# Convolution and feed-forward products over all tokens as 2x2 blocks in seven block products, with the combined operands in SBUF slots and DRAM

## Chip, cores and metric

The kernel runs on one core of a Trainium2 chip. The metric is the device time of one execution in microseconds (us); less is better.

## What is computed

Two blocks follow each other on 1024 tokens of 1024 features. `first_block` (two layers, a gated mixing layer and a windowed attention) ends with the normed residual X2. The change concerns `second_block`, which is run with one layer:

```python
def short_conv_mixer(h, w_in, conv_w, w_out, on_grid):
    gate_b, gate_c, hv = jnp.split(h @ w_in, 3, axis=-1)
    u = gate_c * hv
    conv = conv3_grid(u, conv_w) if on_grid else conv3_seq(u, conv_w)
    return (gate_b * conv) @ w_out
...
def swiglu(h, w_in, w_out):
    gate, up = jnp.split(h @ w_in, 2, axis=-1)
    return (jax.nn.silu(gate) * up) @ w_out
...
        hl = modulate(rmsnorm(x, norm1_g[i]), sh1, sc1)
...
        x = x + g1 * yl
        x = x + g2 * swiglu(modulate(rmsnorm(x, norm2_g[i]), sh2, sc2), ffn_w_in[i], ffn_w_out[i])
...
    return rmsnorm(x, final_g)
```

`w_in` of the convolution is 1024x3072 and `w_out` 1024x1024; the feed-forward layer has 2816 hidden features (22 groups of 128), so its `w_in` is 1024x5632 and its `w_out` 2816x1024. `conv3_grid` is a three-tap convolution within rows of 64 tokens.

## The kernel before

Every large product is made in float32r in three matmuls: each operand is split into a high part (ACT casts it, L100) and a remainder (DVE subtracts, L101), and TensorE (PE) adds high by high, high by remainder and remainder by high into one PSUM bank. Weights come page by page: `wpage` loads 512 KB into one of three `raw` buffers (L115, issued by SP), lets POOL multiply it by a gate row where one is given (L117), and splits it into one of four pages `w`. A page is so ready after a load, a cast and a subtraction.

The second block works in two halves of 512 tokens (`tg`), each over

- conv in (L1145 in `by_feature`): 24 groups of 128 features, each 24 matmuls 128x512 over a page; then, on DVE and ACT, the product of the two gates and the convolution (L1171 to L1180);
- conv out (L1196): four pages for each half of the output features, four tiles of 128 tokens; the residual X2 is loaded (L1200), X3 stored, and for the first half of the tokens the normed and transposed input of the feed-forward layer is built (`to_h3`);
- FFN in (L1145 again): 44 groups of features; L1238 to L1240 make the gated product;
- FFN out (L1285): eleven pages for each half of the output features, `end_of` adds the residual and norms.

The operands of the matmuls (features by tokens, both parts) lie in the large tiles H and HB. The input of conv in is built for tiles 0 to 3 within the attention, and for tiles 4 to 7 by `reload_h2`, as steps spread by `mix` over the conv in products of the first half: X2 is loaded back (L1154), normed (L917 to L933), transposed on PE (L136), shifted (L141, L143) and split.

Each engine has one instruction stream in a fixed order, laid out by a scheduler when the kernel is built; SP issues nearly all DMAs, each behind those ahead of it. The attention ends, tile by tile, with the out products (L983), the layer norm (L987 to L1015, on DVE, ACT and POOL) and the store of X2 (L1016).

## Time and profile before

| | |
|---|---|
| time, median of 3 runs | 2709.77 us (2708.3 to 2711.15) |
| profiled execution, span | 2708.1 us, 36954 instructions |
| PE busy (matmuls) | 2665.1 us, 98% |
| DVE busy | 1639.9 us, 61% |
| ACT busy | 1033.3 us, 38% |
| POOL busy | 519.8 us, 19% |
| HBM traffic | 302.82 MB read, 44.89 MB written |

The span runs from the first to the last instruction of the profiled execution; the median of the runs is 1.7 us above it. PE counts as busy from the issue of a matmul to its modelled end, so overlapping matmuls are counted once.

### The profile page before, as it was taken

How to read it: one execution, taken by the hardware profiler on the slowest of the kernel's cores; microseconds unless marked ns; L12 is line 12 of the kernel's file. 1: busy time of each engine (PE TensorE's matmuls, PEld its weight loads, DVE VectorE, ACT ScalarE, POOL GpSimd, SP SyncE). 2: the span in 40 equal slices, each digit the busy share in tenths (PEclk: the TensorE clock that was granted, in tenths of full speed). 3: DMA queues.
4: the chain of work that ended last, by engine and by line, in shares of the span. 5: the costliest groups of instructions: out<-in, count | busy, mean ns of one | idle time of the engine just before them, and what ended most of it. 6: DMA issues, size and time to landing. Idle time of an engine off the chain costs nothing.

```text
span 2708.1 us, 36954 instructions
## 1 busy us (share of the span) xinstructions
PE 2665.1 (98%) x14170; PEld 2294.9 (85%) x14170; DVE 1639.9 (61%) x2751; ACT 1033.3 (38%) x1839; POOL 519.8 (19%) x522
## 2 busy tenths in 40 slices
PE   8999999999999999999999999999999999999998
PEld 5799998879999788888888888888888888888887
DVE  5677775666778765556677876464444355434443
ACT  4323334322223435345556874342232233222222
POOL 2010000010001412213345761000000034100143
PEclk9999999999999999999999999999999999999999
DMA  7454334464444435541374216253453333433322
GB/s 255 140 151 122 99 119 124 123 206 132 134 137 133 146 97 192 176 155 61 89 247 141 82 64 186 87 163 94 132 156 94 101 102 121 152 98 97 94 94 78
DMA packets 348757, 350.11 MB, mean 129 GB/s; under 512 B 13910, under 2 KB 256110, under 8 KB 348066
## 3 DMA queue, kind: packets, MB, share of 16 engines
q1 hardware_dynamic: 340836, 336.74, 40.2%
q10 hardware_dynamic: 7744, 11.01, 1.1%
q8 instruction: 111, 1.82, 0.3%
q14 instruction: 66, 0.54, 0.1%
HBM read 302.82 MB, written 44.89 MB: 128 GB/s over the span
## 4 chain that ended last, share of the span: by engine, by line
PE 85%; DVE 5%; DMA 4%; ACT 2%; issue 2%; POOL 1%; SPq 0%; POOLq 0%; DVEq 0%; ACTq 0%
PE PS L1145 26%; PE PS L510 14%; PE PS L1285 9%; PE PS L597 7%; PE PS L670 5%; PE PS L386 5%; PE PS L1039 3%; PE PS L1196 3%; PE PS L983 2%; PE PS L855 2%; DMA raw<-in_a_w_in 2%; PE PS L889 2%; PE PS L877 2%; PE PS L491 1%; DVE H L101 1%
## 5 line engine op out<-in xcount | busy, mean ns | idle before, releaser
L101 DVE TENSOR_TENSOR w<-raw,w 128x1024 fp32r<-128x1024 f32 x294 | 411.6, 1401 | 414.6 <-ACT w L100 413.9
L100 ACT CAST w<-raw 128x1024 fp32r<-128x1024 f32 x296 | 310.9, 1051 | 806.8 <-issue 305.0
L1145 PE MATMUL PS<-H,w 128*128 128x512 f32 x2688 | 613.1, 389 | 0.7 <-DVE w L101 0.5
L1145 PEld LDWEIGHTS PS<-H,w 128*128 128x128 f32 x2688 | 503.7, 188 | 105.8 <-DVE w L101 1.0
L510 PE MATMUL PS<-H,w 128*128 128x320 f32 x2112 | 320.5, 309 | 0.8 <-DVE TT L519 0.8
L510 PEld LDWEIGHTS PS<-H,w 128*128 128x128 f32 x2112 | 310.8, 188 | 2.9 <-DVE TT L519 1.1
L117 POOL TENSOR_TENSOR raw<-raw,gb 128x1024 f32<-128x1024 f32 x44 | 111.6, 2536 | 520.6 <-DMA raw<-in_ffn_w_out 500.2
L333 POOL TENSOR_TENSOR H<-ACC,H 128x256 fp32r<-128x256 f32 x52 | 51.4, 988 | 609.4 <-ACT H L332 474.3
L314 DVE SCALAR_TENSOR_TENSOR ACC<-raw,CO,ACC 128x512 f32<-128x512 f32 x182 | 134.2, 749 | 21.1 <-DMA raw<-in_ada_w 18.4
L510 PE MATMUL PS<-H 128*128 128x320 f32 x960 | 144.7, 309 | 0.0
L510 PEld LDWEIGHTS PS<-H 128*128 128x128 f32 x960 | 141.1, 188 | 0.5
L597 PE MATMUL PS<-w,H 128*128 128x512 f32 x600 | 141.3, 394 | 0.1
L1145 PE MATMUL PS<-HB,w 128*128 128x512 f32 x576 | 134.8, 396 | 0.0
L1285 PE MATMUL PS<-w,H 128*128 128x512 f32 x576 | 133.4, 390 | 0.0
L597 PEld LDWEIGHTS PS<-w,H 128*128 128x128 f32 x600 | 112.3, 189 | 23.6 <-ACT TT L515 0.2
L1145 PEld LDWEIGHTS PS<-HB,w 128*128 128x128 f32 x576 | 108.1, 188 | 26.1
L101 DVE TENSOR_TENSOR PTR<-PS,PTR 128x512 fp32r<-128x512 f32 x176 | 106.2, 614 | 38.4 <-ACT PTR L100 37.0
L1285 PEld LDWEIGHTS PS<-w,H 128*128 128x128 f32 x576 | 107.9, 188 | 22.5
L386 PE MATMUL PS<-H 128*128 128x512 f32 x510 | 120.9, 391 | 0.0
L864 ACT ACTIVATE s<-s,sm 128x641 f32<-128x641 f32 (+1 forms) x128 | 103.2, 807 | 43.9 <-DVE sm L862 43.3
L100 ACT CAST PTR<-PS 128x512 fp32r<-128x512 f32 x176 | 91.7, 524 | 57.8 <-PE PS L877 53.7
L386 PEld LDWEIGHTS PS<-H 128*128 128x128 f32 x510 | 94.1, 188 | 21.1 <-issue 0.5
(275 smaller groups left out, 4293.4 us busy)
## 6 DMA issues: line engine op xcount, KB each, us to landing
raw<-in_a_w_in SPq DMA_DIRECT2D x96, 512.0 KB
raw<-in_ffn_w_in SPq DMA_DIRECT2D x88, 512.0 KB
raw<-in_ada_w SPq DMA_DIRECT2D x80, 512.0 KB
raw<-in_conv_w_in SPq DMA_DIRECT2D x48, 512.0 KB
raw<-in_ffn_w_out SPq DMA_DIRECT2D x44, 512.0 KB
raw<-in_a_w_out SPq DMA_DIRECT2D x32, 512.0 KB
raw<-in_b_w_in SPq DMA_DIRECT2D x20, 512.0 KB
VY<-in_ada_w SPq DMA_DIRECT2D x16, 512.0 KB
```

Of the source, the lines that this page charges most:

```text
L100: A.copy(hi, src)
L101: turn["split"] = (eng or V).tensor_tensor(lo, src, hif, ALU.subtract)
L117: G.tensor_tensor(rv, rv, scale, ALU.mult)
L314: V.scalar_tensor_tensor(ACC[:, s, :], r[:, j, :], CO[:, c, k:k + 1], ACC[:, s, :], ALU.mult, ALU.add)
L386: T.matmul(ps, HT[0][:, k, ap, t * 128:(t + 1) * 128], w[:, k % 2, :], start=k == 0 and n == 0, stop=k == 7 and n == 2)
L510: T.matmul(pss[h][:, 0:320], w[:, k, :], HT[0][:, k, ap, h * 320:(h + 1) * 320], start=k == 0 and n == 0, stop=k == 7 and n == 2)
L597: turn["mm"] = T.matmul(accs[t], ys[j].r[:, ap * 640 + t * 128:ap * 640 + (t + 1) * 128], wv[:, j, :], start=kp == 0 and j == 0 and n == 0 ...
L670: T.matmul(pss[j], HP[0][:, g + j, k, ap, :], w[:, k % 2, :], start=k == 0 and n == 0, stop=k == 7 and n == 2)
L864: A.activation(out=p[:, :nk + 1], in_=p[:, :nk + 1], func=AF.Exp, scale=-1.0, bias=sm[:, j:j + 1], accum_out=sm[:, 2 + j:3 + j])
L1039: T.matmul(ps, w[:, k, :], HP[0][:, 2 + 4 * tg:6 + 4 * tg, k, ap, :], start=k == 0 and n == 0, stop=k == 7 and n == 2)
L1145: T.matmul(ps, w[:, k, :], act[:, k, ap, :], start=k == 0 and n == 0, stop=k == 7 and n == 2)
L1285: turn["mm"] = T.matmul(accs[t], hr[:, ap, t * 128:(t + 1) * 128], wv[:, j, :], start=kp == 0 and j == 0 and n == 0, stop=kp == NKP - 1 an ...
```

## The change

Conv in, conv out, FFN in and FFN out are no longer made in halves of 512 tokens, but over all 1024 tokens at once, as products of 2x2 blocks: two groups of features (or two halves of the inner dimension) by two halves of the tokens, in seven block products P1 to P7 in place of eight, in Winograd's form of Strassen's scheme.

- *Right operands.* The blocks B11, B21, B12 and the combinations T1 to T4 of the activations (`right_operands`: four subtractions and five remainder parts on DVE for each pair of tiles) lie in seven slots of 4096 words, five in H and two in HB, for the in products. `keep_half` builds and stores (HR2) the conv input of tiles 0 to 6 within the attention; the last tile is built behind it from the stored X2[7].
- *Left operands.* For two groups of weights, `left_operands` loads two pages into a ring of four raw buffers, makes four combinations on DVE, and splits three and a half pages. `ahead` puts P1 and P2 of the first two sets ahead of the rest.
- *Out products.* The activations of the out products are combined by POOL and written to DRAM (`spill`: TC, TF), those of the weights by POOL steps spread over the in products (`sums_steps`: SC, SF). `out_products` reads both back by `wpage`, seven products in the order P1, P6, P2, P7, P5, P4, P3, into pages that are cut out of the slots. In conv out, what P4 and P3 give is finished by `third`: X3 is stored, normed, transposed, and combined into the slots of FFN in.

The matmuls 128x512 of these four products go from 1152 + 384 + 2112 + 1056 = 4704 to 1008 + 336 + 1848 + 924 = 4116.

```diff
--- before.py
+++ after.py
...
+        HR2 = scratch("HR2", 7, [128, D])
+        HR3 = scratch("HR3", 4, [128, D])
+        RIGHTS = ("B11", "B21", "B12", "T1", "T2", "T3", "T4")
+        TC, TF = ({x: dr.tile([n, 128, 512], F32, name=f"{nm}{x}") for x in RIGHTS} for nm, n in (("TC", 4), ("TF", NFF // 2)))
+        SC, SF = ({x: dr.tile([n, 128, 512], F32, name=f"{nm}{x}") for x in ("S1", "S2", "S3", "S4")}
+                  for nm, n in (("SC", 4), ("SF", NFF // 2)))
...
+        def keep_half(xs, half, i):
...
+            if i < 4:
+                split(H2[0][:, half, 0, :, i * 128:(i + 1) * 128], H2[0][:, half, 1, :, i * 128:(i + 1) * 128],
+                      H2[1][:, half, 0, :, i * 128:(i + 1) * 128], h.rearrange("p (k t) -> p k t", k=4))
+            SY.dma_start(HR2[i][:, half * 512:(half + 1) * 512], h)
...
+        ORDER = ("P1", "P6", "P5", "P7", "P2", "P3", "P4")
+        RIGHT = {"P1": "B21", "P2": "B11", "P3": "B12", "P4": "T4", "P5": "T1", "P6": "T2", "P7": "T3"}
...
+        def split_slots(names, where, t, src):
...
+            for s in range(n):
+                A.copy(r[:, s, 0, :, tk], src[:, s * 512:(s + 1) * 512].rearrange("p (k t) -> p k t", k=4))
+            for s in range(n):
+                V.tensor_tensor(r[:, s, 1, :, tk], src[:, s * 512:(s + 1) * 512].rearrange("p (k t) -> p k t", k=4),
+                                f[:, s, 0, :, tk], ALU.subtract)
+        def right_operands(where, t, h1, h2, tmp):
...
+            split_slots(("B12",), where, t, b12)
+            V.tensor_tensor(t1, b22, b21, ALU.subtract)
+            V.tensor_tensor(t2, b12, t1, ALU.subtract)
+            V.tensor_tensor(t3, b12, b22, ALU.subtract)
+            V.tensor_tensor(t4, b11, t2, ALU.subtract)
+            split_slots(("T1", "T2"), where, t, tmp[:, 0:1024])
+            split_slots(("T3", "T4"), where, t, tmp[:, 1024:2048])
...
+        def left_operands(w, c1, c2):
...
+            r1, r2 = next_raw(), next_raw()
+            SY.dma_start(r1.rearrange("p (k n) -> p k n", k=8), rows(w, c1, 128))
+            SY.dma_start(r2.rearrange("p (k n) -> p k n", k=8), rows(w, c2, 128))
...
+            g1, g2, g3 = page(), page(), page()
...
+            def first():
+                split(g1.r[:, 0:1024], g1.r[:, 1024:2048], g1.f[:, 0:1024], r1)
+            def rest():
+                split(pa[:, 0:512], pa[:, 512:1024], paf[:, 0:512], r2[:, 0:512])
+                a11, a12, a21, a22 = r1[:, 0:512], r1[:, 512:1024], r2[:, 0:512], r2[:, 512:1024]
+                V.tensor_tensor(a21, a22, a21, ALU.add)
+                V.tensor_tensor(a22, a12, a22, ALU.subtract)
+                split(g2.r[:, 0:1024], g2.r[:, 1024:2048], g2.f[:, 0:1024], r2)
+                V.tensor_tensor(a12, a21, a12, ALU.subtract)
+                V.tensor_tensor(a11, a11, a12, ALU.subtract)
+                split(g3.r[:, 0:1024], g3.r[:, 1024:2048], g3.f[:, 0:1024], r1)
...
+        def product(st, name, where, start=True):
...
+            for k in range(4):
+                for n, (w, ap) in enumerate(((hi, 0), (hi, 1), (lo, 0))):
+                    turn["mm"] = T.matmul(ps, w[:, k, :], b[:, ap, k, :], start=start and k == 0 and n == 0,
+                                          stop=k == 3 and n == 2, skip_group_check=not start)
...
+        def tail(st, where, c12):
+            st["rest"]()
+            p1, p5 = st["p1"], U(2 + st["i"] % 2)
+            b = product(st, "P6", where)
+            V.tensor_tensor(p1, b, p1, ALU.add)
+            c = product(st, "P5", where)
+            A.copy(p5, c)
+            G.tensor_tensor(p5, p5, p1, ALU.add)
+            d = product(st, "P7", where)
+            V.tensor_tensor(p5, d, p5, ALU.add)
+            if "early" not in st:
+                product(st, "P2", where, False)
+            c = product(st, "P3", where, False)
+            V.tensor_tensor(c12, c, p1, ALU.add)
+            d = product(st, "P4", where, False)
+            V.tensor_tensor(p1, d, p1, ALU.add)
+            return st["c11"], c12, p1, p5
+        def ahead(sets, where):
+            for st in sets:
+                head(st, where)
+            for st in sets:
+                product(st, "P2", where, False)
+                st["early"] = True
...
+        def spill(dst, j, even, odd, tmp):
...
+            for name, x in (("B11", b11), ("B21", b21), ("B12", b12)):
+                SY.dma_start(dst[name][j], x)
+            G.tensor_tensor(t1, b22, b21, ALU.subtract)
+            SY.dma_start(dst["T1"][j], t1)
+            G.tensor_tensor(t2, b12, t1, ALU.subtract)
+            SY.dma_start(dst["T2"][j], t2)
...
+            def s1():
+                SY.dma_start(a, block(2, 2))
+                SY.dma_start(b, block(2, 1))
+                G.tensor_tensor(a, a, b, ALU.add)
+                SY.dma_start(dst["S1"][j], a)
+                SY.dma_start(b, block(1, 2))
...
+            wpages[:] = pages
+            turn["w"] = 0
+            for name in ("P1", "P6", "P2", "P7", "P5", "P4", "P3"):
...
+                def operands(j, n):
+                    x = right[RIGHT[name]][j:j + n].rearrange("j p t -> p j t")
+                    return wpage(x, n, 512), wpage(moving(name, j, n), n, 512)
...
+                for t in range(4):
+                    use(name, t, ps[:, t])
+                mix.tick()
...
-        H2B = [x.rearrange("p (k h t) -> p k h t", k=8, h=2) for x in (HBt.r, HBt.f)]
-        H3 = H2
...
+        c_in, c_out = I["conv_w_in"][0], I["conv_w_out"][0]
+        first = [left_operands(c_in, 1024 + f * 128, 2048 + f * 128) for f in range(2)]
+        ahead(first, N1)
+        xs = U(4, 2)
+        SY.dma_start(xs, X2[7])
...
+        for t in range(4):
+            a, b = pairs_of()
+            SY.dma_start(a, HR2[t])
+            if t < 3:
+                SY.dma_start(b, HR2[4 + t])
+            else:
+                b = U(16, 2)
+            right_operands(N1, t, a, b, U(12, 4))
...
+            spill(TC, j, cvs[0], cvs[1], U(12, 4))
...
+        def third(i, xs, junk):
...
+            rms(RM[:, i:i + 1], MS[:, i, :])
+            xn, hs = next_raw(), next_raw()
+            V.tensor_scalar(xn, xs, RM[:, i:i + 1], None, op0=ALU.mult)
+            for h in range(2):
+                feature_blocks(xn[:, h * 512:(h + 1) * 512], hs[:, h * 512:(h + 1) * 512], h,
+                               lambda k: C2[:, 24 + k:25 + k], lambda k: C2[:, 16 + k:17 + k], PS[:, 4 + t])
+            if i < 4:
+                split_slots(("B11",), N3, t, hs[:, 0:512])
+                split_slots(("B21",), N3, t, hs[:, 512:1024])
+                SY.dma_start(HR3[t], hs)
+            else:
+                h1 = next_raw()
+                SY.dma_start(h1, HR3[t])
+                right_operands(N3, t, h1, hs, U(8, 4))
+        def conv_use(name, t, ps):
...
+            elif name == "P4":
+                xs = xsr()
+                SY.dma_start(xs, X2[t])
+                G.tensor_tensor(xs[:, 0:512], xs[:, 0:512], r, ALU.add)
+                V.tensor_tensor(r, ps, u2, ALU.add)
+                V.tensor_tensor(r, r, gbs[1], ALU.mult)
+                V.tensor_tensor(xs[:, 512:1024], xs[:, 512:1024], r, ALU.add)
+                third(t, xs, r)
...
+        out_products(c_out, 4, TC, SC, slot_pages((2, 4, 3, 5, 1)), conv_use)
...
+        first = [left_operands(f_in, f * 128, (NFF + f) * 128) for f in range(2)]
+        ahead(first, N3)
...
+                spill(TF, f // 2, ys[0], ys[1], U(12, 4))
...
+        FG = RAW.pop()
...
+        out_products(f_out, NFF // 2, TF, SF, slot_pages((0, 4, 3, 1, 6, 5, 2)), ffn_use)
```

Three places of the new order follow. First PE at the end of the attention, before; `L983` are the attention's out products, `L889` its products with the values, `L1145` conv in, and w_144 to w_147 the four weight pages.

```order
L983 MATMUL PS<-w_146,ot_9555 128x512 x6
L889 MATMUL PS<-PTR,H 128x256 x4
L983 MATMUL PS<-w_147,ot_9555 128x512 x6
L1145 MATMUL PS<-H,w_146 128x512 x24
L1145 MATMUL PS<-H,w_147 128x512 x2
L983 MATMUL PS<-KVA,ot_9555 128x512
L983 MATMUL PS<-w_144,ot_9555 128x512
L1145 MATMUL PS<-H,w_147 128x512 x5
L983 MATMUL PS<-KVA,ot_9555 128x512 x5
L983 MATMUL PS<-w_144,ot_9555 128x512 x5
L1145 MATMUL PS<-H,w_147 128x512 x17
```

After, `L998` are the out products, `L941` transposes of `keep_half`, `L1229` the block products, `L1374` the transposes of the last tile, w_177 to w_180 the weight pages, and slots 5 and 6 (T3, T4) lie in HB:

```order
L998 MATMUL PS<-w_179,ot_9588 128x512 x6
L998 MATMUL PS<-KVA,ot_9588 128x512 x6
L998 MATMUL PS<-w_180,ot_9588 128x512 x6
L998 MATMUL PS<-w_177,ot_9588 128x512 x6
L1229 MATMUL PS<-H,w_180 128x512 x12
L1229 MATMUL PS<-H,w_177 128x512 x12
L941 MATMUL PS<-ident,ZX 128x128 x8
L1229 MATMUL PS<-H,w_177 128x512 x12
L1229 MATMUL PS<-H,w_180 128x512 x12
L1374 MATMUL PS<-ident,E 128x128 x8
L1229 MATMUL PS<-HB,w_178 128x512
```

Before, products of conv in stand between those of the attention; now all of them stand behind the last out product, 48 of them ahead of the last tile's transposes, and the next after those reads T3.

Second, SP behind the attention; before, X_126 is the last tile's X2, X_123 to X_125 those of tiles 4 to 6, r_9554 the tile that it is stored from.

```order
L115 DMA raw_150<-in_conv_w_in 128x8x128 x2
L1016 DMA X_126<-r_9554 128x512 x2
L115 DMA raw_148<-in_conv_w_in 128x8x128
L1154 DMA xs_13840<-X_123 128x1024
L1154 DMA xs_13841<-X_124 128x1024
L1185 DMA gb_13855<-GT_138 128x512
L1200 DMA R_13852<-X_119 128x512
```

After, HR_135 to HR_141 are the stored inputs of tiles 0 to 6 and E the working tile:

```order
L1031 DMA X_126<-r_9587 128x512 x2
L952 DMA HR_141<-ZX 128x512
L1193 DMA raw_13955<-in_conv_w_in 128x8x128
L1365 DMA E<-X_126 128x1024
L1391 DMA E<-HR_139 128x1024
L1391 DMA E<-HR_140 128x1024
L1389 DMA E<-HR_136 128x1024
L1193 DMA raw_182<-in_conv_w_in 128x8x128
L1192 DMA raw_181<-in_conv_w_in 128x8x128
L1193 DMA raw_13955<-in_conv_w_in 128x8x128
L1389 DMA E<-HR_135 128x1024
L1391 DMA E<-HR_141 128x1024
```

The last tile's input comes back from X2 (L1365), and all loads of the others (L1389, L1391) stand behind the store of X2[7] (L1031).

Third, DVE from conv out to FFN in; before, the page splits and gated products (L1239) of FFN in follow the last residual at once.

```order
L101 TENSOR_TENSOR w_147<-raw_150,w_147 128x1024
L1203 TENSOR_TENSOR e_13844<-PS,gb_13856 128x512
L101 TENSOR_TENSOR w_144<-raw_148,w_144 128x1024
L1205 TENSOR_TENSOR r_13854<-e_13844,r_13854 128x512
L920 TENSOR_TENSOR RM<-MS 128x1
L921 TENSOR_SCALAR RM<-RM 128x1
L101 TENSOR_TENSOR w_145<-raw_149,w_145 128x1024
L1239 SCALAR_TENSOR_TENSOR e_13844<-e_13844,PS 128x512
L1240 SCALAR_TENSOR_TENSOR e_13846<-e_13844,PS 128x512
L101 TENSOR_TENSOR w_146<-raw_150,w_146 128x1024
```

After, `L1381` is the shift of the transposed input, `L1169` a remainder part of a slot, `L1177` to `L1180` its combinations, `L1212` to `L1216` those of the weights, `L107` a remainder part of the weights, w_177 the page of the first P1:

```order
L1381 TENSOR_SCALAR raw_183<-PS,C_193 128x128
L1169 TENSOR_TENSOR H<-E,H 128x4x128
L107 TENSOR_TENSOR PA<-raw_182,PA 128x512
L1177 TENSOR_TENSOR E<-raw_183,raw_13955 128x512
L1179 TENSOR_TENSOR E<-raw_183 128x512
L1212 TENSOR_TENSOR raw_182<-raw_182 128x512
L1178 TENSOR_TENSOR E<-raw_183,E 128x512
L1169 TENSOR_TENSOR H<-E,H 128x4x128
L1213 TENSOR_TENSOR raw_182<-raw_181,raw_182 128x512
L107 TENSOR_TENSOR w_177<-raw_181,w_177 128x1024
L1180 TENSOR_TENSOR E<-raw_13955,E 128x512
L1169 TENSOR_TENSOR H<-E,H 128x4x128 x2
```

The split of the page that P1 of FFN in reads now stands behind the shifts and nearly all combinations of the last four tiles.

## Rows read from the trace of the kernel before

**Rows 1.** The page's parts 1 and 2: engine shares, and the granted clock.
```profile
PE 2665.1 (98%) x14170; PEld 2294.9 (85%) x14170; DVE 1639.9 (61%) x2751; ACT 1033.3 (38%) x1839; POOL 519.8 (19%) x522
...
PEclk9999999999999999999999999999999999999999
```

**Rows 2.** Windows of the second block: length, busy time by engine, clock, DMA share, GB/s.
```profile
1800.00:2000.00 200.00, 200.00 (x871) 162.66 (x870) 99.22 (x134) 60.71 (x87) 3.20 (x5) 1.00 0.45 134
...
2200.00:2400.00 200.00, 200.00 (x893) 164.54 (x892) 98.44 (x107) 60.22 (x90) 53.24 (x24) 1.00 0.41 127
```

**Rows 3.** Waits of PE from 1640 us to the end: total, times, longest.
```profile
PE PS L136 <- DVE xs L933: 1.8, 1, 1.8
```

**Rows 4.** Timeline of PE around the end of the attention: start, length, line, count.
```profile
1593.55 3.11 PE L1145 MATMUL PS<-H,w 128*128 128x512 f32 x13
...
1624.04 1.33 PE L983 MATMUL PS<-w,ot 128*128 128x512 f32 x5
1625.20 26.94 PE L1145 MATMUL PS<-H,w 128*128 128x512 f32 x118
1653.98 1.09 PE L136 MATMUL PS<-ident,xs 128*128 128x128 f32 x8 [1.84 <-DVE xs L933]
```

**Rows 5.** Line L1145: shortest, median and longest matmul in ns.
```profile
L1145 PE MATMUL PS<-H,w x2688: 387/389/506, 1593.5 to 2579.2; 128*128 128x512 f32 x192
```

**Rows 6.** DVE's groups by shape, 1600 to 2708 us: busy time, mean ns.
```profile
L101 DVE TENSOR_TENSOR w<-raw,w 128x1024 fp32r<-128x1024 f32 x195 | 278.3, 1428 | 330.4 <-ACT w L100 330.0 <-PE PS L1196 0.4
L1240 DVE SCALAR_TENSOR_TENSOR e<-e,PS 128x512 f32<-128x512 f32 x44 | 30.3, 688 | 106.4 <-PE PS L1145 106.3
L101 DVE TENSOR_TENSOR H<-e,H 128x512 fp32r<-128x512 f32 x40 | 27.5, 687 | 8.1 <-ACT H L100 7.9
L143 DVE TENSOR_SCALAR hs<-PS,C 128x128 f32<-128x128 f32 x48 | 18.6, 405 | 15.5 <-PE PS L136 15.0 <-ACT hs L141 0.3
L933 DVE TENSOR_SCALAR xs<-xs,SM 128x1024 f32<-128x1024 f32 x4 | 3.0, 752 | 2.0 <-POOL SM L922 2.0
```

**Rows 7.** POOL's groups by shape, 1600 to 2708 us.
```profile
L1014 POOL TENSOR_TENSOR r<-r,H 128x512 f32<-128x512 f32 x6 | 8.0, 1350 | 6.4 <-ACT r L1013 6.4
```

**Rows 8.** Timeline at the end of the attention: what releases the last tiles.
```profile
1626.31 0.68 DVE L987 CUSTOM_DVE_ANT_0 r<-PS,r 128x512 f32<-128x512 f32 x1
...
1641.22 1.76 SPq L1016 DMA_DIRECT2D X<-r  x2
...
1643.56 1.66 SPq L1154 DMA_DIRECT2D xs<-X  x2
...
1650.35 0.63 ACT L917 ACTIVATE hs<-xs 128x512 f32<-128x512 f32 x1 [8.65 <-DMA xs<-X]
...
1653.18 0.74 DVE L933 TENSOR_SCALAR xs<-xs,SM 128x1024 f32<-128x1024 f32 x1
```

**Rows 9.** Timeline of the first layer's end: a store of 512 KB, and its reader.
```profile
1091.32 0.32 SPq L652 DMA_DIRECT2D X1A<-xs  x1
...
1093.92 0.32 SPq L654 DMA_DIRECT2D xs<-XH  x1
```

**Rows 10.** Timeline of FFN out: a page's load, and POOL beside DVE.
```profile
2236.69 5.08 SPq L115 DMA_DIRECT2D raw<-in_ffn_w_out  x2
...
2239.07 1.05 ACT L100 CAST w<-raw 128x1024 fp32r<-128x1024 f32 x1 [0.21 <-PE PS L1285]
2240.15 1.23 DVE L101 TENSOR_TENSOR w<-raw,w 128x1024 fp32r<-128x1024 f32 x1 [0.48 <-ACT w L100]
2240.49 3.15 POOL L117 TENSOR_TENSOR raw<-raw,gb 128x1024 f32<-128x1024 f32 x1 [4.91 <-DMA raw<-in_ffn_w_out]
...
2245.14 2.42 POOL L117 TENSOR_TENSOR raw<-raw,gb 128x1024 f32<-128x1024 f32 x1 [1.50 <-DMA raw<-in_ffn_w_out]
2245.76 2.87 DVE L101 TENSOR_TENSOR w<-raw,w 128x1024 fp32r<-128x1024 f32 x1 [4.38 <-ACT w L100]
```

**Rows 11.** Timeline of PE, first layer: a wait and the products behind it.
```profile
54.13 2.50 PE L386 MATMUL PS<-w,H 128*128 128x512 f32 x5 [3.66 <-DVE H L101]
```

**Rows 12.** Windows around that wait (columns as in rows 2).
```profile
54.00:56.00 2.00, 1.86 (x4) 1.50 (x5) 2.00 (x5) 1.80 (x6) 0.00 (x0) 0.50 0.62 156
...
58.00:60.00 2.00, 2.00 (x13) 1.28 (x12) 0.18 (x1) 0.44 (x3) 0.00 (x0) 0.65 0.65 239
60.00:62.00 2.00, 2.00 (x19) 1.37 (x17) 1.69 (x3) 2.00 (x3) 0.00 (x0) 1.00 0.02 8
```

**Rows 13.** Timeline of the tail: the last products, and the last store's issue.
```profile
2699.45 1.56 PE L1285 MATMUL PS<-w,HX 128*128 128x512 f32 x6
```

More of the change, by code (lines that the diff above doesn't have):

```diff
@@ L922, in rms @@
             G.tensor_tensor(dst, dst, mhalf[:, 0:1], ALU.pow)
-        def into(h, t):
-            return lambda k0, n: tuple(x[:, k0:k0 + n, j, t * 128:(t + 1) * 128]
-                                    for x, j in ((h[0], 0), (h[0], 1), (h[1], 0)))
         def normed_h2(i, xs, dst, hsr):
@@ new lines, in head @@
+        def head(st, where):
+            st["first"]()
+            st["p1"] = U(st["i"] % 2)
+            ps = product(st, "P1", where)
+            A.copy(st["p1"], ps)
+            st["c11"] = ps
+        def tail(st, where, c12):
[15 more added lines that the diff above has]
+            return st["c11"], c12, p1, p5
@@ new lines, in program @@
+        cvr = ring([U(4 + 2 * i, 2) for i in range(3)])
+        steps = [x for j in range(4) for x in sums_steps(c_out, j, SC, U(16), U(17))]
+        mix.begin(steps, 11)
+        for j in range(4):
+            cvs = []
+            for f in (2 * j, 2 * j + 1):
+                if f < 2:
+                    st = first[f]
+                else:
+                    st = left_operands(c_in, 1024 + f * 128, 2048 + f * 128)
+                    head(st, N1)
+                u, cv = U(10, 2), cvr()
+                c11, c12, c21, c22 = tail(st, N1, u[:, 512:1024])
+                V.tensor_tensor(u[:, 0:512], c11, c21, ALU.mult)
+                V.tensor_tensor(u[:, 512:1024], c12, c22, ALU.mult)
+                V.tensor_scalar(cv, u, cw[:, 8 + f:9 + f], None, op0=ALU.mult)
@@ new lines, in program, with fourth @@
+        mix.end()
+        FG = RAW.pop()
+        turn["raw"] = 0
+        SY.dma_start(FG, I["final_g"].partition_broadcast(128))
+        for m in range(2):
+            SY.dma_start(gbs[m], GT[4][m, :].partition_broadcast(128))
+        xsr = ring([U(12, 2), U(14, 2)])
+        late = [U(12, 2), U(14, 2), U(8, 2), U(10, 2)]
+        def fourth(i, xs):
+            rms(RX[:, i:i + 1], MS[:, i, :])
+            for h in range(2):
+                c = slice(h * 512, (h + 1) * 512)
+                V.scalar_tensor_tensor(xs[:, c], xs[:, c], RX[:, i:i + 1], FG[:, c], ALU.mult, ALU.mult)
+                SQ("l").dma_start(out[0, i * 128:(i + 1) * 128, c], xs[:, c])
```

395 lines of the change are left out of this document (227 added, 168 removed).

## Prediction

> **What bounds the kernel now.** I read the page's shares first: PE is busy for 98% of the span, DVE for 61, and the granted clock stands at the upper of its two levels, 2.4 GHz, in all forty slices [rows 1]. An average over stages does not tell what the second block alone is bound by, so the windows come next: from 1800 to 2400 us PE is busy without a gap, while DVE has half its time free, POOL a quarter at most in use, and the DMAs move 127 to 134 GB/s [rows 2]. The waits of PE from 1640 us to the end agree: the longest is 1.8 us [rows 3]. The second block is bound by the count of its matmuls, and whatever else it does is hidden.
>
> What a matmul is worth must be read with care. Its own record says 389 ns [rows 5], but matmuls overlap: 118 of them take 26.94 us [rows 4], that is 0.2283 each; I use 0.2285. The second block's 4704 matmuls are then 1075 us.
>
> The end of the attention is the place at which other work is covered. 55 conv in matmuls stand there between the attention's own from 1593.55 us on (13 in the first of six such rows), and the last out product ends at T0 = 1625.2 [rows 4]. Behind T0 the span is accounted for: 4649 matmuls (1062.3), twelve groups of eight transposes like the one at 1653.98 (1.03 each, 12.4), and 8.2 of waits and tail. The tail is 7.1 of these, from the end of the last products (2701.0) to 2708.1 [rows 13].
>
> **Removed.** 588 matmuls, 134.4 us. This is the whole gain. By the record's 389 ns it would be 229, which the row of 118 excludes. From T0 on 4116 are left instead of 4649: -121.8. T0 itself: the 55 matmuls (12.6) can no longer stand ahead of it, since P1's pages are the last two that the out products use; three more groups of transposes for tiles 4 to 6 enter (+3.3), and I give 2.3 for the attention's own short waits that the 55 filled: T0 moves by -7 (bounds -12.6 and 0). The 12.4 of transposes behind T0 now fall into the waits below, and the old 8.2 goes out, to be put in anew.
>
> **Added: three places where PE waits for DVE.** Before, all that feeds the next products was spread under products of the other half of the tokens. With all tokens in one product that cover is gone: nothing of conv in beyond P1 and P2 of two sets can run before the last tile is there, and so at each turn. The prices are those of DVE's steps: 0.687 for a 128x512 subtraction, 0.405 for a shift, 0.75 for a scaling of 128x1024 [rows 6], and 1.23 for a page's remainder when POOL is idle [rows 10].
>
> *Attention to conv in.* The 48 matmuls ahead take 11 us, so PE runs dry at about T0 + 13. The last tile's chain of before: its sums start 1.1 us behind T0, its store is issued at 1641.22, T0 + 16; the load behind it is issued at 1643.56 and lands at 1650.35, 6.8 us later, and the tile is scaled by 1653.9 [rows 8]. A store is followed by its reader after 2.6 us [rows 9]. After, with no page splits of conv in between, I put the store at T0 + 14, the load at +16.6, its landing at +23.4, the scaled tile at +27, and the shifted features at +31 (transposes 1.1, four shifts on DVE for each pair of halves, ACT beside it). `right_operands` is nine DVE steps for each of four pairs, 36; by the order six stand ahead of that point and 30 behind: 20.6 us, to +51.6. The stored tiles' loads stand behind the last store on SP and go into two working pairs, so that the second use of a pair waits for the first: one load of 6.8, nearly all of it, shows: +6, to +57.6. The matmuls that come next read T3 of all tiles, so PE starts there: a wait of 45 us (bounds 36, without the loads and with the store at +12, and 55, with two loads).
>
> *P4 to P3 in conv out.* `third` of tiles 0 to 3 stands ahead of P3 on PE by its 32 transposes, and it borrows the raw buffers that P3's pages need. For each tile DVE makes three steps on the product (2.07), the scaling (0.75), four shifts (1.62), two remainders (1.37) and two small ones (0.3): 6.1, with four tiles and P3's four pages 29.4 us. P3 has only 11 us of matmuls, and ends 43.5 behind P4's end T4 instead of 11: 33 us (bounds 25, if POOL's and ACT's links and the loads into the raws are all covered, and 40).
>
> *Conv out to FFN in.* `third` of tiles 4 to 7 is 4.7 + 6.2 (`right_operands`) = 10.9 us of DVE each, 43.7 in all; with two sets of left operands 56.7 stand in the order from P3's results to the last split that the first sets need. The split that P1 waits for (w_177) comes after 44.2 of them. Some 8 us run before P3 ends, and ACT, POOL and the loads of HR3 add 2: P1 starts at 38 if DVE is undisturbed. It is not: POOL has about 13 steps here, six or seven of which I let DVE wait for.
>
> How much that costs, the trace shows: a remainder of a page takes 1.23 us when POOL starts behind it, and 2.87 when it runs beside POOL's product of 2.42 [rows 10]; the mean over all is 1.43 [rows 6]. POOL's 128x512 step takes 1.35 [rows 7]. DVE reads PSUM in the gated product and stays at 0.688 [rows 6]. I take 8 us, so a wait of 46 (bounds 38 and 56: no collision, or all 13 in full). The Trainium skill, "SBUF — State Buffer", section "Who interferes with whom", says that a DVE step with two SBUF inputs and a GpSimd step that reads SBUF exclude each other for a whole instruction; the 2.87 agrees. By that rule all 13 could count, 56, against the 46 that I take from the mean of the rows.
>
> **Added: smaller terms.** The clock: after a wait of 3.66 us five matmuls take 2.50 us [rows 11], and the windows show 0.50 of full speed, 1.2 GHz, from 54 us, 0.65 until 60, then full speed [rows 12]; some 2.6 us are lost at each restart, three times 8 (bounds 0 and 16). Behind the first and third wait DVE still has left operands to make, 7.1 us a set (3 x 1.23 and 5 x 0.687); I let PE wait 4 of it twice, 8 (bounds 0 and 14). FFN out begins with pages whose load (2236.69 to 2240.49, 3.8), cast (1.05) and remainder (1.23) [rows 10] sum to 6.1; half of it shows, 3. The tail has two scalings in a row on DVE and two more steps in place of one: 8.5. Conv in to conv out has its first pages ready: nothing, covered by 11 us of matmuls for each P.
>
> The in products themselves: a set is 84 matmuls, 19.2 us of PE. DVE has 14.6 us in a gate set of the convolution and 12.6 in one of FFN in (three page remainders and thirteen steps of 0.687), so PE stays the bound if POOL's four to five steps a set cost DVE no more than 4.6 to 6.6 us. They come to 5 to 6.7 when each is waited for in full; with the rows' mean they cost half. I allow 4 us in all.
>
> **The sum** against the profiled span: 2708.1 - 7 - 121.8 - 12.4 - 8.2 = 2558.7; with 45 + 33 + 46 it is 2682.7; with 8 + 8 + 3 + 8.5 + 4 it is 2714.2. The median lies 1.7 above the span, so 2716. The change gives back in three waits what the seventh product saves.
>
> **Rivals.**
> *DVE is undisturbed and early (faster).* The links beside DVE's own counted work (loads of the stored tiles in the first wait, raws in the second, POOL in the third) are all covered, since loads can be issued early and POOL's steps can fall into DVE's waits for ACT. For it speaks that of 195 page remainders the mean is only 0.2 above the free 1.23. Price: 45 becomes 42.5, 33 becomes 25, 46 becomes 38: 2716 - 18.5 = 2697. It decides from where the three waits sum to less than 112 us, 12 below my 124.
> *POOL makes DVE the bound in the in products.* If each POOL step costs DVE its 1.35 and one cast of 1.05 shows in each set, a set of FFN in is 12.6 + 6.75 + 1.05 = 20.4, 1.2 above PE's, 26 over 22 sets; the eight gate sets, 14.6 + 5 + 1.05, add 11: 2716 - 4 + 37 = 2749. For it speaks the 2.87; against it, that PSUM readers, half of DVE's steps, stay at their price.
> *FFN out is paced by the loads.* It has 84 pages, twelve for each P, at twice the pace of before, on three buffers. A buffer goes round in 3.8 + 1.05 + 1.23 and some 0.3, 6.3 us, so twelve pages of a P take 25 us against PE's 30.2. With loads of 6.8, as at the end of the attention [rows 8], it is 9.4 and 38: 8 for each of seven P, less what the first pages bring, +53: 2769. Against it: at 127 GB/s the load took 3.8, and FFN out needs some 190.
> *The waits are hidden after all* and the plain saving stays: 2575. The order speaks against it: PE has no products to put there.
>
> **How the numbers follow.** The forecast 2716 (its own range 2704 to 2732) has 0.38, DVE early 0.32, POOL as the bound 0.17, loads 0.10, the plain saving 0.03. No change means within 0.2%, 2704.4 to 2715.2, about what a measurement of this kernel can tell. Of the forecast 0.13 falls within it and 0.25 above; of DVE early 0.28 below and 0.04 within; with the others: faster 0.31, same 0.17, slower 0.52. The range: all three waits at their lower bounds (99) and no clock or slip term give 2716 - 25 - 16 = 2675, the loads as pace 2769; I take 2672 to 2771, which leaves out the plain saving and the far ends of the waits.
>
> **What the profile after would show.** PE with three gaps of some 45, 33 and 46 us, each ended by a DVE remainder part (a slot's in the first, a page's in the others), the granted clock low behind each; 0.2285 us a matmul between them; PE's share down to about 94%; POOL busier by some 100 us. Wrong would be: gaps of less than 30 (the order does not bind where I think), a string of short waits for DVE in FFN in (POOL as the bound), waits for loads in FFN out, or a clock that stays low for longer than the few microseconds behind a gap.

## The result, and the profile after

The changed kernel takes 2787.54 us (median of four runs, 2781.8 to 2789.81) against 2709.07 before: a ratio of 1.0284, with an interval of 1.0269 to 1.0298. The forecast was 2716, with a range of 2672 to 2771. The profiled execution is the fastest of the four, 2781.8 us with a span of 2780.0.

From the page of the changed kernel, the busy times of the engines and the granted clock in forty slices; for the kernel before these are [rows 1]:

```profile
PE 2575.1 (93%) x13582; PEld 2206.0 (79%) x13582; DVE 1881.4 (68%) x3075; ACT 1080.5 (39%) x1911; POOL 675.0 (24%) x660
...
PEclk9999999999999999999999979999769999999997
```

PE has lost 90 us of busy time and five points of its share, POOL has gained 155 us, and the granted clock now dips. Where PE waits from 1600 us on (total, times, longest):

```profile
PE PS L1229 <- DVE E L1251: 35.1, 11, 7.8
PE PS L1374 <- DVE raw L1445: 20.3, 7, 9.0
PE PS L1374 <- ACT raw L1379: 17.1, 7, 7.2
PE PS L1229 <- ACT HB L1167: 15.6, 1, 15.6
PE PS L1229 <- ACT w L106: 14.2, 2, 12.1
PE PS L1335 <- ACT H L106: 13.9, 2, 11.8
...
PE PS L998 <- ACT ZX L946: 3.7, 3, 1.9
PE PS L941 <- DVE ZX L934: 2.6, 1, 2.6
```

Before, the longest of these waits was 1.8 us [rows 3], and the next was

```profile
PE PS L1196 <- ACT hs L141: 1.4, 1, 1.4
```

The largest sum now, 35.1 us behind DVE's L1251, is none of the three waits of the forecast: 24.7 of it stand in FFN in and 10.4 in conv in. PE's timeline shows where each stands (idle time and what ended it in brackets; rows chosen from 1620 us on):

```profile
1621.55 3.27 PE L998 MATMUL PS<-w,ot 128*128 128x512 f32 x12
...
1639.20 7.35 PE L1229 MATMUL PS<-H,w 128*128 128x512 f32 x24 [7.44 <-ACT E L1238]
...
1655.17 1.97 PE L1374 MATMUL PS<-ident,E 128*128 128x128 f32 x8 [8.63 <-DVE E L1370]
1672.70 1.22 PE L1229 MATMUL PS<-HB,w 128*128 128x512 f32 x2 [15.56 <-ACT HB L1167]
...
1771.50 5.01 PE L1229 MATMUL PS<-HB,PA 128*128 128x512 f32 x12 [7.85 <-DVE E L1251]
...
1963.12 16.51 PE L1335 MATMUL PS<-H 128*128 128x512 f32 x72
...
2013.42 3.33 PE L1335 MATMUL PS<-H 128*128 128x512 f32 x6 [11.79 <-ACT H L106]
...
2025.83 1.54 PE L1335 MATMUL PS<-HB 128*128 128x512 f32 x6
...
2070.78 1.22 PE L1229 MATMUL PS<-H,w 128*128 128x512 f32 x2 [12.10 <-ACT w L106]
...
2134.54 4.45 PE L1229 MATMUL PS<-H,PA 128*128 128x512 f32 x12 [2.85 <-DVE E L1251]
...
2204.10 5.42 PE L1229 MATMUL PS<-H,PA 128*128 128x512 f32 x12 [4.50 <-DVE E L1251]
...
2361.70 2.96 PE L1229 MATMUL PS<-H,PA 128*128 128x512 f32 x12
...
2380.98 2.96 PE L1229 MATMUL PS<-H,PA 128*128 128x512 f32 x12
```

The last two rows are the same product of two successive sets of FFN in, behind all waits: a set then takes 19.28 us. Cut at the places where one group of products ends and the next begins, the span compares with the forecast as follows. The forecast's column is its own sum, stretch by stretch, with 2.6 us for the clock put beside each of the three waits; the last column is an experiment that is told below.

| stretch | matmuls x 0.2285 | forecast | measured | all mends |
|---|---|---|---|---|
| to the last out product of the attention | | 1618.2 | 1624.7 | 1628.3 |
| conv in, with the wait ahead of it | 230.3 | 281.9 | 286.4 | 275.5 |
| conv out, with the wait ahead of P3 | 76.8 | 112.4 | 116.3 | 118.1 |
| wait for P1 of FFN in | | 48.6 | 43.4 | 37.3 |
| FFN in | 422.3 | 430.3 | 467.5 | 430.0 |
| FFN out | 211.1 | 214.1 | 209.9 | 208.9 |
| tail, from the last product | | 8.5 | 31.9 | 18.2 |

The stretches with the three waits came within 5 us of the forecast, though the first of them by two errors that cancel (see below). Two stretches did not: FFN in (37 us more; some 35 if the clock's 2.6 behind the third wait are counted here, where they fell) and the tail (23). They are what the experiments are about.

### The profile page after: what moved, and what is told of

It is laid out like the page before. It is cut to its first block, busy times and chain, and to the rows that moved or that the text cites. A ratio compares the mean times of both kernels' runs of the same rounds, so it can differ in the third digit from the quotient of the medians.

```text
span 2780.0 us, 36848 instructions
## 1 busy us (share of the span) xinstructions
PE 2575.1 (93%) x13582; PEld 2206.0 (79%) x13582; DVE 1881.4 (68%) x3075; ACT 1080.5 (39%) x1911; POOL 675.0 (24%) x660
## 4 chain that ended last, share of the span: by engine, by line
PE 63%; DMA 16%; DVE 8%; POOL 5%; ACT 4%; issue 3%; SPq 1%; POOLq 0%; DVEq 0%; ACTq 0%
PE PS L516 15%; PE PS L1229 13%; PE PS L603 7%; PE PS L392 6%; PE PS L676 5%; DMA E<-in_ffn_w_out 4%; PE PS L1053 3%; PE PS L998 3%; PE PS L861 2%; PE PS L1335 2%; PE PS L895 2%; PE PS L883 2%; DMA raw<-SFS 2%; DVE H L107 2%; DMA E<-in_conv_w_out 2%
## 5 line engine op out<-in xcount | busy, mean ns | idle before, releaser
L1229 PE MATMUL PS<-H,w 128*128 128x512 f32 x1776 | 418.1, 393 | 22.4 <-ACT w L106 14.2
L1229 PEld LDWEIGHTS PS<-H,w 128*128 128x128 f32 x1776 | 336.7, 190 | 96.1 <-ACT w L106 15.4
L106 ACT CAST w<-raw 128x1024 fp32r<-128x1024 f32 x202 | 211.5, 1050 | 396.7 <-PE PS L1229 140.9
L107 DVE TENSOR_TENSOR w<-raw,w 128x1024 fp32r<-128x1024 f32 x200 | 266.7, 1338 | 117.2 <-ACT w L106 115.8
L516 PEld LDWEIGHTS PS<-H,w 128*128 128x128 f32 x2112 | 310.8, 188 | 3.0 <-DVE TT L525 1.2
L107 DVE TENSOR_TENSOR H<-raw,H 128x1024 fp32r<-128x1024 f32 (+1 forms) x133 | 166.4, 1262 | 123.0 <-ACT H L106 121.1
L1335 PE MATMUL PS<-H 128*128 128x512 f32 x924 | 216.0, 392 | 14.0 <-ACT H L106 13.9
L106 ACT CAST H<-raw 128x1024 fp32r<-128x1024 f32 (+1 forms) x133 | 134.1, 1018 | 233.0 <-DMA raw<-in_a_w_in 68.8
L1335 PEld LDWEIGHTS PS<-H 128*128 128x128 f32 x924 | 173.8, 189 | 52.7 <-ACT H L106 14.7
L1229 PE MATMUL PS<-HB,w 128*128 128x512 f32 x672 | 166.7, 401 | 16.7 <-ACT HB L1167 15.6
L1229 PEld LDWEIGHTS PS<-HB,w 128*128 128x128 f32 x672 | 128.0, 191 | 48.3 <-ACT HB L1167 16.0
L320 DVE SCALAR_TENSOR_TENSOR ACC<-raw,CO,ACC 128x512 f32<-128x512 f32 x182 | 133.8, 747 | 20.5 <-DMA raw<-in_ada_w 17.8
L516 PEld LDWEIGHTS PS<-H 128*128 128x128 f32 x960 | 141.1, 188 | 0.5
L603 PE MATMUL PS<-w,H 128*128 128x512 f32 x600 | 140.0, 391 | 0.1
L1251 DVE TENSOR_TENSOR E<-PS,E 128x512 f32<-128x512 f32 x34 | 23.5, 691 | 162.9 <-POOL E L1249 121.9
L107 DVE TENSOR_TENSOR PTR<-PS,PTR 128x512 fp32r<-128x512 f32 x176 | 106.2, 613 | 36.5 <-ACT PTR L106 35.0
L603 PEld LDWEIGHTS PS<-w,H 128*128 128x128 f32 x600 | 111.5, 188 | 23.4 <-ACT TT L521 0.2
L392 PE MATMUL PS<-H 128*128 128x512 f32 x510 | 120.9, 391 | 0.0
```

The lines of the kernel that those rows point to most:

```text
L106: A.copy(hi, src)
L107: turn["split"] = (eng or V).tensor_tensor(lo, src, hif, ALU.subtract)
L320: V.scalar_tensor_tensor(ACC[:, s, :], r[:, j, :], CO[:, c, k:k + 1], ACC[:, s, :], ALU.mult, ALU.add)
L392: T.matmul(ps, HT[0][:, k, ap, t * 128:(t + 1) * 128], w[:, k % 2, :], start=k == 0 and n == 0, stop=k == 7 and n == 2)
L516: T.matmul(pss[h][:, 0:320], w[:, k, :], HT[0][:, k, ap, h * 320:(h + 1) * 320], start=k == 0 and n == 0, stop=k == 7 and n == 2)
L603: turn["mm"] = T.matmul(accs[t], ys[j].r[:, ap * 640 + t * 128:ap * 640 + (t + 1) * 128], wv[:, j, :], start=kp == 0 and j == 0 and n == 0 ...
```

## Experiments

A kernel was run once in most of them, on chips on which the kernel before took 2708 to 2715 us; so the stretches are compared rather than the totals. In the runs that leave a stretch as it was it still varies: FFN in from 467.4 to 471.4 us, the tail from 31.4 to 34.5.

### FFN in: three theories of one wait

The windows of the changed kernel show that the loss is in the part of FFN in in which the weight sums are made (columns as in [rows 2]):

```profile
2120.00:2340.00 220.00, 195.35 (x797) 156.90 (x796) 121.91 (x156) 56.13 (x75) 85.53 (x61) 0.94 0.57 184
2340.00:2500.00 160.00, 160.00 (x699) 130.80 (x698) 117.02 (x134) 51.17 (x69) 36.66 (x24) 1.00 0.32 106
```

Until 2340 us PE is idle for 25 us; behind that, when the last sums are stored, it is busy throughout. What stands ahead of the wait at 2204.10, from the timeline of all engines:

```profile
2196.07 1.29 POOL L1291 TENSOR_TENSOR E<-E 128x512 f32<-128x512 f32 x1 [5.61 <-DMA E<-in_ffn_w_out]
...
2200.84 1.26 POOL L1296 TENSOR_TENSOR E<-E 128x512 f32<-128x512 f32 x1 [3.48 <-DMA E<-in_ffn_w_out]
2202.06 1.26 POOL L1249 TENSOR_TENSOR E<-E 128x512 f32<-128x512 f32 x1
...
2203.36 0.69 DVE L1251 TENSOR_TENSOR E<-PS,E 128x512 f32<-128x512 f32 x1 [10.30 <-POOL E L1249]
```

L1249 adds P5 and P6 of the set in hand. It stands on POOL behind two steps of the weight sums (L1291, L1296) that each wait for a load; DVE's L1251 waits 10.30 us for it, holds up all that is behind it on DVE, and PE waits for the bank that L1251 reads. The theories: A, this order on POOL's queue; B, the port that DVE and POOL share; C, SP's queue, on which weight pages stand behind stores that wait for POOL.

**P5's sum on DVE.**

```diff
-            G.tensor_tensor(p5, p5, p1, ALU.add)
+            V.tensor_tensor(p5, p5, p1, ALU.add)
```

> Only the sum of the fifth product and the sixth (one 128x512 addition for each set of the in products, L1249) goes from POOL to DVE. Theory A (POOL's queue): that sum stands on POOL behind steps of the weight sums that wait for their loads, so DVE's addition behind it, and PE's next product in that bank, wait for a load that has nothing to do with them; the waits of PE for DVE's L1251 (35 us in the profile after) vanish, with what the clock loses behind them: about 40 us less, a span of 2736 to 2745. Theory B (shared port): DVE loses its time to POOL's steps, which all remain, and DVE gets 34 more steps of 0.69: no gain, 2778 to 2790. Theory C (SP's queue: the weight pages come late behind stores that wait): no gain either.

The span is 2755.2 us. FFN in takes 449.9 instead of 467.5, conv in 279.9 instead of 286.4; PE's waits behind L1251 fall to

```profile
PE PS L1229 <- DVE E L1251: 15.0, 5, 4.2
```

The gain of 25 us in all lies between what A expected (40) and what B and C did (none). A holds for 17.6 us of FFN in, but not for all: 26 us above 22 sets of 19.28 stay.

**Weight sums without POOL's additions.**

```diff
-                G.tensor_tensor(a, a, b, ALU.add)
+                if add:
+                    G.tensor_tensor(a, a, b, ALU.add)
```

(the same for the three subtractions; `add` is false in the feed-forward layer.)

> In the feed-forward layer the sums of the weights are not added on POOL: the loads and stores remain in their order, the 44 additions are left out (the output is then of other weights). Theory A (POOL's queue behind loads): nothing on POOL waits for those loads any more, so FFN in runs at PE's 19.3 us a set: about 32 us less, 2745 to 2752. Theory B (shared port): the same 44 steps are gone, 44 x 1.3 us of DVE's waits at most: 20 to 35 less. Theory C (SP's queue): the stores still wait on SP for their loads, ahead of the weight pages: less than 10 us gained. This run tells C from the others, the run with the sum on DVE tells A from B.

The span is 2755.3 us, above A's 2745 to 2752, as conv out took 6 us longer in this run; FFN in takes 434.5, 33 less. A and B both allow that. What C expected did not come, but without additions a store on SP no longer waits for POOL either, so the run is no clear test of C.

**The weight sums' DMAs on POOL's queue, besides P5's sum on DVE.**

```diff
-                SY.dma_start(dst["S1"][j], a)
-                SY.dma_start(b, block(1, 2))
+                G.dma_start(dst["S1"][j], a)
+                G.dma_start(b, block(1, 2))
...
```

> As the run with the sum of P5 on DVE, and the loads and stores of the weight sums are issued by POOL in place of SP. With the sum on DVE FFN in still took 449.9 us from its first to its last product, against 424 for 22 sets at 19.28. Theory C (SP's queue: the weight pages wait behind the sums' stores, which wait for POOL): FFN in takes 424 to 432, and conv in loses a few us too. Theory B (shared port): no change against 450, since all steps of POOL remain.

The span is 2754.0 us. Conv in gains 7 more (273.1), FFN in nothing (454.7), which looked like B. The wait for P1 of FFN in fell as well, to 37.2 us; no run here tells why. But the waits of SP, ACT and PE in FFN in speak against B:

```profile
SPq L1279 <- POOL E L1278: 134.1, 6, 27.9
...
ACT w L106 <- DMA raw<-in_ffn_w_in: 67.2, 6, 16.1
...
PE PS L1229 <- ACT E L1238: 12.7, 4, 3.9
```

SP now stands up to 27.9 us before the stores of `spill`, whose combinations (L1278) are behind the sums on POOL, and ACT waits up to 16.1 us for weight pages that SP has not yet asked for. Behind these casts on ACT stands its copy of P1 (L1238), and PE waits for the bank that this copy reads.

**The stores of `spill` on POOL's queue too.** This was run on the kernel with the feed-forward part alone (below), whose FFN in is the same, and in the kernel with all mends.

```diff
-                SY.dma_start(dst[name][j], x)
+                G.dma_start(dst[name][j], x)
...
-            SY.dma_start(dst["T1"][j], t1)
+            G.dma_start(dst["T1"][j], t1)
```

> The mended feed-forward kernel, and the stores of the combined activations (spill) are issued by POOL too, so that nothing but weight pages stands on SP in FFN in. There FFN in still took 453 us for 22 sets of 19.28 (424), and SP waited 115 us for the first of POOL's combinations. Theory C (SP's queue): 424 to 435. Theory B (shared port, or DVE's and ACT's own work): 445 or more.

FFN in falls from 453.4 us (457.4 in another run of the same FFN in, on the chip of this run) to 431.1. ACT's waits for weight pages of FFN in, ahead of this step (the largest row) and behind it (the only one left):

```profile
ACT w L104 <- DMA raw<-in_ffn_w_in: 65.4, 6, 16.6
```

```profile
ACT PA L104 <- DMA raw<-in_ffn_w_in: 1.9, 1, 1.9
```

C is shown for this part, and B is not the bound: POOL's steps all remain. Each of these gains is that of a step in this order; the stores of `spill` were not moved alone.

### The tail

**The late residuals into the raw buffers.**

```diff
-        late = [U(12, 2), U(14, 2), U(8, 2), U(10, 2)]
+        late = [None, None, None, U(8, 2)]
...
+                if t == 0:
+                    for q in range(4):
+                        if q < 3:
+                            late[q] = next_raw()
```

> In FFN out the residual tiles of the last four tiles of tokens are loaded into the three raw buffers, free once P3's last pages are split, and one working tile, instead of tiles that P4's last results hold until they are stored. Theory D (buffers): the 31.9 us from the last product to the end are a chain of loads that wait for buffers (the last three loads are issued 5 to 11 us behind the last product): 10 to 18 us less, 2762 to 2770. Theory E (work): DVE's and POOL's steps of the last eight tiles alone fill the tail: less than 5 us gained, 2775 to 2781.

The tail is 26.9 us, 5 less, between D and E (the span, 2785.5, has other differences of several us ahead of it and lies above both). The loads that now came late were those of P4's third and fourth tile.

**Four residual tiles for P4 as well.**

```diff
-        xsr = ring([U(12, 2), U(14, 2)])
+        xsr = ring([U(12, 2), U(14, 2)] + XT)
...
```

(XT are two tiles in the space of PA; the late residuals are in the raw buffers, as above.)

> As the run with the residuals in raw buffers (late tiles in the raw buffers), and PA's 2048 words, idle in FFN out, become two more residual tiles, so that P4's four tiles no longer share two. That run left a tail of 26.9 us, in which the loads of P4's third and fourth tile were issued only behind the stores of the first two. Theory D' (P4's ring of two sets the tail): from the last product to the end 10 to 16 us, against 31.9 in the changed kernel. Theory E (work of DVE and POOL): 22 or more.

The tail is 25.0 us, against an expectation of 10 to 16 by theory D': the buffers were not the main part. DVE's timeline shows where else to look:

```profile
2739.45 1.29 DVE L107 TENSOR_TENSOR H<-raw,H 128x512 fp32r<-128x512 f32 x2
...
2740.65 1.28 DVE L1559 TENSOR_TENSOR E<-PS,E 128x512 f32<-128x512 f32 x2
```

DVE comes to the first of P4's results (L1559) only when the last page of P3 is split (L107), 17 us before the last product, and has eight tiles to finish from there.

**P3's last pages behind P4's steps.**

```diff
-                got = [(j, n, *operands(j, n)) for j, n in last]
+                with tc.issue_after(turn["p4"].ins) if last and "p4" in turn else nullcontext():
+                    got = [(j, n, *operands(j, n)) for j, n in last]
```

> The mended feed-forward kernel, and in FFN out the remainder parts of P3's last pages are queued on DVE behind the three steps of each of P4's tiles, which stood behind all of P3's pages: there DVE came to P4's results some 8 us before PE was done though they had been ready for 20, and worked on eight tiles until the end. Theory H (the order of DVE's queue makes the tail): the tail falls from 24.1 us to 10 to 16. Theory E (DVE's work on the last four tiles fills it in any order): 20 or more. If P3's last pages come late instead, FFN out grows beyond 209 by what the tail loses.

The tail is 20.5 instead of 24.1 us, at the end that theory E gave; FFN out stays at 208.9. DVE came to P4's results 28 us ahead of the last product instead of 22 (not 8, as the expectation had it). With `spill` on POOL's queue the same edit takes the tail from 23.4 to 17.0. So the buffers are worth 7 to 10 us (31.9 to 25.0 here, 34.5 to 24.1 in the feed-forward kernels below) and the order 4 to 6. The rest is argued, not tested: in the tail of 17.0 us DVE works on the last tiles for 11.8 us, nearly without a wait, and the last stores land behind that. In the kernel with both parts and all mends the tail is 18.2 us; it was never brought to the 8.5 of the forecast.

### What sets the third wait

**Without the remainder parts of the last four tiles.**

```diff
-            for s in range(n):
+            for s in range(n if lo else 0):
                 V.tensor_tensor(r[:, s, 1, :, tk], src[:, s * 512:(s + 1) * 512].rearrange("p (k t) -> p k t", k=4),
```

> Between conv out and FFN in, the 20 remainder parts (five for each of the last four tiles, 0.687 us each, 13.7 us of DVE) of the combined right operands are left out; those parts of the slots keep old values. Theory F (DVE's counted work sets this wait, as predicted): the stretch from P3's last product to P1 of FFN in shrinks from 43.6 us by 11 to 14. Theory G (the chain of loads, transposes and ACT steps sets it, and DVE's steps lie beside): it shrinks by less than 5.

The wait for P1 falls from 43.4 to 34.8 us: 8.6 for 13.7 us of DVE's work left out, between the two theories.

```profile
2028.56 1.54 PE L1335 MATMUL PS<-HB 128*128 128x512 f32 x6
...
2064.91 1.22 PE L1229 MATMUL PS<-H,w 128*128 128x512 f32 x2 [10.69 <-ACT w L106]
```

DVE's steps are part of this chain, but not all of it; ACT's shifts end some of PE's waits between conv out's P4 and FFN in (17.1 us in the list above). What sets the first two waits was not tested by a run.

### One part alone, and all mends

**The feed-forward part alone.** Conv in and conv out are those of before, in halves of tokens; the input of FFN in is put into the slots tile by tile behind each product of conv out (the edit is shown against the kernel before).

```diff
...
+        N3 = {"B21": 0, "B11": 1, "B12": 2, "T1": 5, "T2": 6, "T3": 3, "T4": 4}
...
         for tg in range(2):
             for fc in range(8):
                 gb_, gc_, hv_ = [by_feature(rows(c_in, base + fc * 128, 128), (H2B if tg else H2)[0]) for base in (0, 1024, 2048)]
...
+                        to_h3(xs, t, tg)
...
```

> One part alone: conv in and conv out as before the change, in halves of 512 tokens; FFN in and FFN out by seven block products. 396 of the 588 matmuls are saved. By the ledger of the changed kernel: 2708 - 90.5 (396 x 0.2285), + 46 for the wait between conv out and FFN in and its clock, + 44 for FFN in behind the weight sums, + 24 for the tail: 2731 (2715 to 2745). Rival (the wait is as dear as all three together, since conv out's last half now carries the work): 2760 or more.

The time is 2719.27 us (the kernel before on that chip 2713.06), within the range expected. FFN in (474.6) and the tail (34.5) lose as in the changed kernel, but the wait ahead of P1 is only 16.8 us, not 46: the next tile's 24 matmuls run while DVE combines the last one.

**The same with the first mends** (P5's sum on DVE, the sums' DMAs on POOL's queue, the residual tiles).

> The feed-forward part alone by block products, with three mends: the sum of P5 on DVE, the weight sums' DMAs on POOL's queue, four residual tiles and the late ones in raw buffers in FFN out. If the causes named so far are the whole loss: 2708 - 90.5 + 46 + 5 + 6 = 2675 (2665 to 2690), 20 to 40 us faster than the kernel before. If the losses only move elsewhere: 2700 or more.

The time is 2687.08 us, near the upper end of what was expected; FFN in was still 453.4, which led to the run with the stores of `spill`.

**Both parts, all mends.**

> The changed kernel with all mends: P5's sum on DVE, all DMAs of the weight sums and of the combined activations on POOL's queue, four residual tiles and late ones in the raw buffers, and P3's last pages behind P4's steps. If its excess over the forecast lay in these queues: 2780 less 13 in conv in, 6 at the third wait, 15 to 35 in FFN in, 8 to 18 in the tail, that is 2708 to 2738, no faster than the kernel before, since three waits remain. Rival (the waits, too, came from the queues): below 2700.

The span is 2716.3 us and the time 2718.12, 0.3% above the kernel before (2710.32 on that chip); its stretches are the last column of the table. In FFN in PE is now idle nowhere between 2120 and 2340 us, with POOL and DVE busier than in the changed kernel:

```profile
2120.00:2340.00 220.00, 220.00 (x959) 179.89 (x958) 186.46 (x197) 67.75 (x91) 128.41 (x153) 1.00 0.57 179
```

**The feed-forward part alone, all mends.**

> Feed-forward part alone with all mends: 2687 less what the two runs beside it gain (8 to 14 in the tail, 0 to 25 in FFN in): 2650 to 2680, 1.2 to 2.4 per cent faster than the kernel before.

The time is 2658.93 us (median of four runs, 2657.71 to 2662.0) against 2710.32: a ratio of 0.9813, interval 0.9796 to 0.9829. It is the fastest version here, 1.9% faster than the kernel before. From its page, the busy times of the engines, and its one long wait:

```profile
PE 2582.1 (97%) x13774; PEld 2221.8 (84%) x13774; DVE 1844.1 (69%) x3001; ACT 1067.2 (40%) x1891; POOL 664.2 (25%) x769
```

```profile
1997.54 5.06 PE L1220 MATMUL PS<-H,w 128*128 128x512 f32 x11 [16.83 <-ACT E L1354]
```

## Why the prediction was wrong

**The step that failed** is "I allow 4 us in all" for the in products. It asked only whether DVE and POOL have enough time in a set, and they have. It did not ask what stands behind what on the queues. The trace before had no step on POOL that waits for a load while PE waits for POOL's next step: in FFN out a multiplied page is a page that PE needs anyway. The change put both on one queue, and its stores ahead of the weight pages on SP. FFN in took 37 us more than forecast: six waits of PE for L1251, 24.0 us, and some 12 for the clock behind them. P5's sum on DVE gave back 17.6, the stores of `spill` off SP's queue 22 to 26, and with both, and the sums' DMAs on POOL's queue, PE had no wait left and FFN in took 430.0. That this is the forecast's 430.3 to a us is luck: the forecast had allowed 8 us for DVE, and what stands there is mostly the clock behind the third wait.

The prediction's own sign of this, "a string of short waits for DVE in FFN in", did appear, but not for the reason of the rival that it stood for. That rival priced POOL's steps (26 us for FFN in); in the kernel with all mends the same steps run and PE does not wait.

**The second** is the tail of 8.5 us, worked out from one tile's chain of before. In the changed kernel P4 and P3 leave eight tiles to the end, since each holds four banks until its last page. 31.9 were measured; buffers and the order of DVE's queue explain a part, and the work of these tiles probably the rest.

**T0 was moved by 0.5 us and not by 7.** From 1200 us to T0 the waits of PE sum to 17.7 us against 10.4 before, 7.3 more, where I had set 2.3; 6.3 stand at the added transposes (the last two rows of the list of waits). That leaves 1.5 of the 6.5 us open, less than the 4 us by which T0 varies between the runs with this attention (1624.7 to 1628.5). No run tests it.

**The first wait was smaller, and conv in came out right by luck.** PE waited 32.8 us in four pieces in place of the one of 45, below its lower bound of 36, and the first product with T3 started 48 us behind T0 instead of 58. But 10.4 us behind L1251 in conv in, and more restarts of the clock than one, made up for it: 286.4 against 281.9. With these waits mended conv in took 275.5. The 48 matmuls ahead did not run in one go, as the forecast had them: behind the first 24 PE waited 7.44 us for ACT's copy of P1 (L1238), which itself waited for the store of X2[7]:

```profile
1638.56 1.07 ACT L1238 COPY E<-PS 128x512 f32<-128x512 f32 x2 [1.19 <-DMA X<-r]
```

**What held.** The other two waits: from P4's end to P3's 48.1 us against 43.5 (of which the counted steps and P3's own matmuls give only 40; the prediction shows no row for the rest), and 43.4 and 2.1 us for FFN in against 46. Their last and longest pieces, 11.79 and 12.10 us, were ended by ACT's casts (L106), not by a DVE remainder part as forecast; in the third, DVE's remainder parts were worth 8.6 us of their 13.7. The price of a matmul: FFN out's 924 took 209.9 us. That FFN out is not paced by loads: PE does not wait there.

The shared port as the bound did not come true: with POOL busy for 128 of 220 us and DVE for 186, PE had no wait. The port does cost DVE time. From 2080 to 2500 us of the changed kernel the 14 steps of L1213 that no step of POOL overlapped took 0.69 us, the six beside one 1.66 to 1.67, and L1255, which reads PSUM, took 0.68 beside POOL too. That PSUM readers keep their price the prediction had taken from a stretch in which POOL hardly worked. One such pair:

```profile
2188.70 1.76 POOL L1307 TENSOR_TENSOR E<-E 128x512 f32<-128x512 f32 x1 [6.40 <-DMA E<-in_ffn_w_out]
...
2189.35 1.66 DVE L1213 TENSOR_TENSOR raw<-raw,raw 128x512 f32<-128x512 f32 x1
2191.04 0.69 DVE L1215 TENSOR_TENSOR raw<-raw,raw 128x512 f32<-128x512 f32 x1
```

The Trainium skill, "SBUF — State Buffer", section "Who interferes with whom", states that a DVE step with two SBUF inputs contends with a GpSimd (POOL) step that reads SBUF, by an exclusive lock. These rows agree. Over 2120 to 2500 us the mean is (busy time, mean ns), against 0.687 us [rows 6]:

```profile
L1213 DVE TENSOR_TENSOR raw<-raw,raw 128x512 f32<-128x512 f32 x18 | 18.3, 1016 | 0.6
```

The clock: three restarts were counted; six more, behind the waits of 2.85 to 5.61 us in FFN in, cost 1.6 to 2.7 us each. The kernel with all mends has a span of 2716.3 against the forecast's sum of 2714.2, but this nearness is luck as well: its T0 and its tail are 10 us above the forecast each and conv out 6, the wait for P1 11 below, conv in 6 and FFN out 5.

**Where the gain went.** Of 134 us saved, the three waits and their clock take some 125 (forecast: 132), and the queues and the tail the rest and 70 more. The feed-forward part alone, with all mends, keeps 52 of its 90 us; its wait of 16.8 us, 10 us in FFN in above the price of its matmuls and a tail 10 us longer take nearly all the rest. Adding the convolution saves 44 us more of matmuls, and yet the kernel with both parts is 60 us slower than the feed-forward part alone, by two more waits and a longer third one. The convolution alone was not run.

## What to carry to other kernels

Where a change gives an engine side work that waits for DMAs, list what is behind it on the same queue, and move either the side work's waits or the step that the critical engine needs to another queue: time free on an engine says nothing about its order. Fewer products paid here only where the other work between two layers still had products to hide under, so try such a scheme part by part: with the same mends, one layer gained 1.9% and both together lost 0.3% (2.8% without the mends).
